# First feed-forward weights loaded through the projections' weight ring, with the token sums' helper tiles moved to other buffers

## The chip, the cores and the metric

The kernel runs on one core of one Trainium2 chip. The metric is device time of one execution in microseconds (us), the median of several runs. TensorE (PE) multiplies, VectorE (DVE) and ScalarE (ACT) do the elementwise work, GpSimd (POOL) a few small operations, and the DMAs of this kernel are issued by SyncE's queue (SP). In this kernel each engine takes its own instructions in the order of its list and waits on semaphores of the others; DMAs are waited for in the same way.

## What is computed

One decoder block on 512 tokens with 1024 channels, float32:

```
h  = rms_norm(x) ;  p = h @ w_in          (split into the parts of two mixers)
yA = sparse attention(p) ; yB = mLSTM(p)
x  = x + (sigmoid(gA) * (yA @ w_branch_a) + sigmoid(gB) * (yB @ w_branch_b)) @ w_out
h2 = rms_norm(x)
x  = x + square(relu(h2 @ w_ff1)) @ w_ff2   (w_ff1: 1024 x 4096, w_ff2: 4096 x 1024)
```

The change lies at the seam between the third and the last line: the end of `@ w_out`, the second norm, and the first columns of `h2 @ w_ff1`.

## The kernel before, in words

**Products in three matmuls.** To keep float32 precision every operand is split into a high part in the reduced format `float32r` and a low part that holds the rest. `split` (L119) does it: ACT writes the high part, DVE subtracts it from the source to get the low part. `mm3` (L114) multiplies high by high, high by low and low by high into one accumulator, so every product is three matmuls.

**Who sets the order.** The order of TensorE's instructions is the program's own (from `es_man` on): generators yield after each product, and `mix` (L260) calls events at given points of the stream. The order on ACT, DVE, POOL and SP is set by the scheduler when the program is built; then it is fixed. Tiles come from pools; a tile with `bufs=n` has n buffers that are used in turn, and who writes a buffer waits until the last reader of its former tile is done. Pools are stacked on two sides of the on-chip memory; closing a pool frees its space for the next.

**The ring.** `load_w` (L95) loads all weights of the projections up to `w_out`: one DMA of up to 512 KB into a `wraw` buffer (3 in the ring), ACT casts it to `whi`, DVE subtracts to `wlo` (4 buffers each). `hidden` (L652) also borrows a `wraw` buffer.

**The output projection.** `out_proj(c)` (L989) computes the 512 channels of half c for four tiles of 128 tokens: 8 steps of k, each `mm3`, so 24 matmuls of 512 columns a tile. Its weights are four ring tiles with two k each. After each token tile of half 1 come the residual add (L1007, DVE), the sum of squares (L1009, ACT), and `norm2` (L974): a reduce on DVE, a power on POOL, two multiplies into `hn` on DVE. `norm2_T` (L980) then transposes `hn` on TensorE (8 matmuls, tile `tpn`), splits it into `hT_h` and `hT_l` and keeps a float32 copy in `hF` (ACT, L154). It is called for token tiles 0 and 1 inside the output projection, for 2 and 3 inside the first feed-forward part.

**The feed-forward part.** The ring is closed (L1019) and four pools are opened: `ffa` (split forms of weights), `ffr` (two 512 KB landing buffers, tag `raw`), `ffu` (13 buffers `u` of [128, 1024]) and `fft` (token sums). `first_ff1` (L1050) computes the first four blocks of 128 hidden channels directly. `load_first` (L1040) loads its weights, 4 DMAs of 512 KB into the two `raw` buffers, and puts high and low parts (`w1h`, `w1l`) into `u` buffers. The products run over tokens 0 to 255 for blocks 0 to 3, then over tokens 256 to 511: 2 x 4 x 8 products, 192 matmuls of 256 columns. The events of its stream are `norm2_T(2)`, then `norm2_T(3)` and `tokens`, then `first_pair`, `load_next(6)` and `tokens4`.

All later blocks go in pairs by a seven-product scheme over halves of channels and tokens: `tokens` (L1068) forms the sums T1, T2, T3 and T4 (the last in the place of `hT`) of the normed tokens in `hF`, and the weights of a pair are turned into the forms a, s, t and b by `w1_a`, `w1_s`, `w1_t`, `w1_b` (L1104 to L1119). `products` (L1122) is `do1` to `do7`, each 12 matmuls of 256 columns: `do1` uses form a, `do2` form s with T2, `do3` form s with T1, `do4` form t with T3, then b with tokens, t with tokens, b with T4. `first_pair` (L1232) makes the forms of blocks 4 and 5; their landing tiles `w1r` and sums `w1s` are `u` buffers, those of later pairs lie in the freed `yb` pool. `ev_u` (L1033) squares and splits a finished block into a `u` buffer. `merge` (L1245) puts the second layer's `unit` (L1205: three matmuls of 512 columns, tile `fo`) between these products. Its weights come by `w2_load` (L1194): a DMA into the two `raw` buffers of `ffr`, a cast to `w2h`, a subtraction to `w2l`.

Of the kernel before, what the change touches and what calls it, by code (L numbers as in the profile page):

```python
# [20 lines left out]
S = 512  # L21
# [31 lines left out]
def hybrid_block_kernel(  # L53
# [30 lines left out]
    yb_l = ybpool.tile([128, ML_H, S], F32R, name="yb_l", tag="yb_l")  # L84
    es_ring = ExitStack()
    ring = es_ring.enter_context(pool("ring", side="right"))

    def acc(name, tag="pj", bufs=2):
        return ps.tile([128, 512], F32, name=name, tag=tag, bufs=bufs)
# [5 lines left out]
    def load_w(src, kn, c0, cn, k0=0):  # L95

        parts, kk = [], 4 if 4 * cn <= 1120 else 2
        for k in range(k0, k0 + kn, kk):
            raw = ring.tile([128, 1120], F32, name="wraw", tag="wraw", bufs=3)
            hi = ring.tile([128, 1120], F32R, name="whi", tag="whi", bufs=4)  # L100
            lw = ring.tile([128, 1120], F32R, name="wlo", tag="wlo", bufs=4)
            n = kk * cn
            nc.sync.dma_start(raw[:, :n].rearrange("p (k c) -> p k c", k=kk), src[:, k:k + kk, c0:c0 + cn])
            nc.scalar.copy(hi[:, :n], raw[:, :n])  # L104
            nc.vector.tensor_sub(lw[:, :n], raw[:, :n], hi.bitcast(F32)[:, :n])  # L105
            parts.append((hi[:, :n].rearrange("p (k c) -> p k c", k=kk),
                          lw[:, :n].rearrange("p (k c) -> p k c", k=kk)))

        def at(k, c=slice(0, cn)):
            h, l = parts[k // kk]  # L110
            return h[:, k % kk, c], l[:, k % kk, c]
        return at
# [6 lines left out]
    def split(h, l, src, scale=1.0):  # L119
        nc.scalar.activation(h, src, AF.Copy, scale=scale)  # L120
        nc.vector.tensor_sub(l, src, h.bitcast(F32))  # L121
# [530 lines left out]
    def hidden(kv, c):  # L652

        w1 = (cmp_k_w1, cmp_v_w1)[kv][0].rearrange("(k p) c -> p k c", p=128)
        raw = ring.tile([128, 1120], F32, name="wraw", tag="wraw", bufs=3)
        hi = cmpp.tile([128, 2, 256], F32R, name="w1h", bufs=3)
        lw = cmpp.tile([128, 2, 256], F32R, name="w1l", bufs=3)
        rv = raw[:, :512].rearrange("p (k c) -> p k c", k=2)
        nc.sync.dma_start(rv, w1[:, 2 * c:2 * c + 2])
        split(hi, lw, rv)  # L660
        if c == 0:
            hacc[kv] = acc("ph", "s", 2)
        p = hacc[kv]

        def go():
            for k in (2 * c, 2 * c + 1):
                lhs = fss[kv][:, k].rearrange("p a g n -> p (a g n)")
                nc.tensor.matmul(p[:, :256], lhs, hi[:, k % 2], start=k == 0, stop=False)
                nc.tensor.matmul(p[:, :256], lhs, lw[:, k % 2], start=False, stop=k == 15)
        return go  # L670
# [345 lines left out]
    esy.close()  # L1016
    qyp.close()

    es_ring.close()  # L1019

    with pool("ffa") as fa, pool("ffr") as fr, pool("ffu") as fu, pool("fft") as ft:
        UB = 13
        us = {}

        def utile(name, dt=F32R):  # L1030
            return fu.tile([128, 2 * S], dt, name=name, tag="u", bufs=UB)

        def ev_u(f, r):  # L1033

            u = utile("u").rearrange("p (a t) -> p a t", a=2)
            nc.scalar.activation(r, r, AF.Square)
            split(u[:, 0], u[:, 1], r)
            us[f] = u

        def load_first(f):  # L1040
            parts = []
            for k in (0, 4):
                raw = fr.tile([128, 4, 256], F32, name="w1raw", tag="raw", bufs=2)
                nc.sync.dma_start(raw, w_ff1[:, k:k + 4, 128 * f:128 * f + 256])
                h, l = (utile("w1" + c).rearrange("p (k c) -> p k c", k=4) for c in "hl")
                split(h, l, raw)
                parts.append((h, l))
            return lambda k, c: (parts[k // 4][0][:, k % 4, c], parts[k // 4][1][:, k % 4, c])

        def first_ff1():  # L1050

            ws = [load_first(0), load_first(2)]
            ps_ = [acc("pj", ("pj", "o")[f // 2], 2) for f in range(4)]
            for hs in (slice(0, 256), slice(256, 512)):
                for f in range(4):
                    for k in range(KT):
                        mm3(ps_[f][:, hs], *ws[f // 2](k, slice(128 * (f % 2), 128 * (f % 2) + 128)),
                            hT_h[:, k, hs], hT_l[:, k, hs], k == 0, k == KT - 1)
                        yield 3 * 256 / 2400
                    if hs.start:  # L1060
                        r = x2p.tile([128, D], F32, name="hn", bufs=2)[:, :S]
                        nc.scalar.activation(r, ps_[f], AF.Relu)
                        ev_u(f, r)
# [27 lines left out]

        def w1_load(f, first=False):
            if first:
                raw, ss = ([utile(n, F32).rearrange("p (k c) -> p k c", k=4) for _ in range(2)] for n in ("w1r", "w1s"))
            else:
                raw, ss = (ybpool.tile([128, 2, 4, 256], F32, name=n, tag=t) for n, t in (("w1r", "yb_h"), ("w1s", "yb_l")))
                raw, ss = [raw[:, 0], raw[:, 1]], [ss[:, 0], ss[:, 1]]
            for i in range(2):
                nc.sync.dma_start(raw[i], w_ff1[:, 4 * i:4 * i + 4, 128 * f:128 * f + 256])
            return raw, ss  # L1100
# [11 lines left out]

        def w1_t(w):
            (r0, r1), (sa, sb) = w
            V.tensor_sub(sb[:, :, one], r0[:, :, one], r0[:, :, two])
            V.tensor_sub(sb[:, :, two], r1[:, :, one], sa[:, :, two])
            form("t", 256, sb)

        def w1_b(w):  # L1119
            form("b", 256, w[0][1])  # L1120

        def products(f, w, nxt):  # L1122

            B = {11: (0, hi_), 21: (4, hi_), 22: (4, lo_)}
            bank = {c: acc("pj", t, 2) for c, t in (("X", "pj"), ("Y", "pj"), ("Z", "o"), ("W", "o"))}
            tmp = x2p.tile([128, 4, 256], F32, name="g2", tag="g2")
            r = x2p.tile([128, 2, S], F32, name="hn", tag="hn", bufs=2)
            X, Y, Z, W_ = (bank[c][:, :256] for c in "XYZW")
            p1, u2, t5 = tmp[:, 0], tmp[:, 1], tmp[:, 2]
            cs = {"a": one, "s1": one, "s2": two, "t3": one, "t4": two, "b1": one, "b2": two}  # L1130

            def prod(o, a, b, start):
                h, l = forms[a[0]]
                c = cs[a]
                for k in range(4):
                    if b in T:
                        bh, bl = T[b][0][:, k], T[b][1][:, k]
                    else:
                        k0, sl = B[b]
                        bh, bl = hT_h[:, k0 + k, sl], hT_l[:, k0 + k, sl]  # L1140
                    mm3(o, h[:, k, c], l[:, k, c], bh, bl, start and k == 0, k == 3, skip_group_check=not start)

            def do1():
                prod(X, "a", 11, True)
                nc.scalar.copy(p1, X)

            def do2():
                prod(Y, "s2", 2, True)
                V.tensor_add(u2, Y, p1)

            def do3():
                prod(Z, "s1", 1, True)
                V.tensor_add(t5, Z, u2)
                if w:
                    w1_a(w)
                    w1_s(w)

            def do4():
                prod(W_, "t3", 3, True)
                V.tensor_add(r[:, 1, lo_], W_, t5)  # L1160

            def do5():
                prod(X, "b1", 21, False)
                nc.scalar.activation(r[:, 0, hi_], X, AF.Relu)

            def do6():
                prod(Z, "t4", 22, False)
                V.tensor_add(r[:, 0, lo_], Z, u2)
                nc.scalar.activation(r[:, 0, lo_], r[:, 0, lo_], AF.Relu)
                ev_u(f, r[:, 0])  # L1170
                if w:
                    w1_t(w)

            def do7():
                prod(W_, "b2", 4, False)
                V.tensor_add(r[:, 1, hi_], W_, u2)
                nc.scalar.activation(r[:, 1], r[:, 1], AF.Relu)
                ev_u(f + 1, r[:, 1])
                if w:
                    w1_b(w)  # L1180
                nxt()

            return [do1, do2, do3, do4, do5, do6, do7]
# [53 lines left out]
        def after_norm():  # L1237
# [2 lines left out]

        mix(Stream(first_ff1()), [(1.54, lambda: norm2_T(2)), (7.32, after_norm), (11.0, first_pair),
                                  (21.0, lambda: load_next(6)), (21.1, tokens4)])
        n2 = iter(order2)

        def merge(fs, n, lead=0):  # L1245
# [48 lines left out]
```

## Time and profile before

| | us |
|---|---|
| three runs, median (lowest to highest) | 812.01 (811.14 to 812.54) |
| the profiled execution, whole | 809.97 |
| its span, first to last instruction | 808.2 |
| PE busy in the span | 787.5 (97%) |
| DVE busy | 536.3 (66%) |
| ACT busy | 407.3 (50%) |
| POOL busy | 71.4 (9%) |

Besides this summary the profile has a timeline of each engine (start, duration, operation, and in brackets how long the engine idled before it and for whom), a list of waits, tables of stretches with each engine's busy time and the clock that TensorE was granted (1.00 is 2.4 GHz, 0.50 is 1.2 GHz), and for each DMA the time from issue to landing. Times on a timeline count from the start of the span. Matmuls overlap: the step from start to start is what one costs in a stream. The profiled execution is 2.0 us shorter than the median of the three timed runs, and of its 809.97 us 1.8 lie outside the span.

### The profile page before, as it was taken

How to read it: one execution, taken by the hardware profiler on the slowest of the kernel's cores; microseconds unless marked ns; L12 is line 12 of the kernel's file. 1: busy time of each engine (PE TensorE's matmuls, PEld its weight loads, DVE VectorE, ACT ScalarE, POOL GpSimd, SP SyncE). 2: the span in 40 equal slices, each digit the busy share in tenths (PEclk: the TensorE clock that was granted, in tenths of full speed). 3: DMA queues.
4: the chain of work that ended last, by engine and by line, in shares of the span. 5: the costliest groups of instructions: out<-in, count | busy, mean ns of one | idle time of the engine just before them, and what ended most of it. 6: DMA issues, size and time to landing. Idle time of an engine off the chain costs nothing.

```text
span 808.2 us, 12445 instructions
## 1 busy us (share of the span) xinstructions
PE 787.5 (97%) x4772; PEld 697.3 (86%) x4772; DVE 536.3 (66%) x1007; ACT 407.3 (50%) x746; POOL 71.4 (9%) x150
## 2 busy tenths in 40 slices
PE   6999999999999999999999989999999999999998
PEld 5978889998888888888888789999998999989886
DVE  6689796778676657764754588677665767664332
ACT  6556564554466656664423576445444444444311
POOL 2000000322122221321000000000000000000000
PEclk9999999999999999999999999999999999999999
DMA  8633231666132123212332241423233333331141
GB/s 308 195 105 92 65 105 49 191 209 182 53 92 79 52 67 92 65 53 79 124 135 68 65 157 56 137 95 105 83 101 105 105 105 105 105 105 53 53 153 56
DMA packets 66320, 84.91 MB, mean 105 GB/s; under 512 B 4063, under 2 KB 50471, under 8 KB 66132
## 3 DMA queue, kind: packets, MB, share of 16 engines
q1 hardware_dynamic: 66168, 84.03, 33.2%
q8 instruction: 37, 0.61, 0.3%
q14 instruction: 23, 0.19, 0.1%
q10 hardware_dynamic: 92, 0.09, 0.0%
HBM read 81.98 MB, written 4.75 MB: 107 GB/s over the span
## 4 chain that ended last, share of the span: by engine, by line
PE 89%; DMA 4%; DVE 3%; ACT 2%; issue 1%; POOL 1%; SPq 0%; DVEq 0%; ACTq 0%; POOLq 0%
PE pj L115 18%; PE pj L116 18%; PE pj L117 18%; PE fo L115 7%; PE fo L117 7%; PE fo L116 7%; PE ao L911 3%; PE tpP L894 2%; PE st L874 1%; PE st L873 1%; DMA bt<-rel_d 1%; DMA w2r<-in_w_ff_dram 1%; PE tpn L149 1%; PE mo L431 1%; PE mo L430 1%
## 5 line engine op out<-in xcount | busy, mean ns | idle before, releaser
L115 PE MATMUL fo<-w2h,u 128*128 128x512 f32 x256 | 100.9, 394 | 0.0
L117 PE MATMUL fo<-w2h,u 128*128 128x512 f32 x256 | 100.2, 391 | 0.0
L116 PE MATMUL fo<-w2l,u 128*128 128x512 f32 x256 | 100.0, 391 | 0.0
L115 PE MATMUL pj<-whi,hT_h 128*128 128x256 f32 (+2 forms) x288 | 84.3, 293 | 3.5 <-ACT hT_h L120 1.8
L105 DVE TENSOR_TENSOR wlo<-wraw,whi 128x1024 fp32r<-128x1024 f32 (+2 forms) x58 | 72.1, 1243 | 21.7 <-ACT whi L104 20.7
L117 PE MATMUL pj<-whi,hT_l 128*128 128x256 f32 (+2 forms) x288 | 82.2, 286 | 0.0
L116 PE MATMUL pj<-wlo,hT_h 128*128 128x256 f32 (+2 forms) x288 | 81.9, 284 | 0.0
L115 PE MATMUL pj<-hT_h,whi 128*128 128x512 f32 x192 | 80.7, 420 | 0.4 <-DVE vv L121 0.4
L116 PE MATMUL pj<-hT_l,whi 128*128 128x512 f32 x192 | 75.9, 395 | 0.0
L117 PE MATMUL pj<-hT_h,wlo 128*128 128x512 f32 x192 | 75.7, 395 | 0.0
L104 ACT CAST whi<-wraw 128x1024 fp32r<-128x1024 f32 (+2 forms) x58 | 60.9, 1050 | 27.9 <-PE pj L116 12.7
L121 DVE TENSOR_TENSOR w2l<-w2r,w2h 128x1024 fp32r<-128x1024 f32 x32 | 39.2, 1223 | 50.1 <-ACT w2h L120 50.1
L120 ACT ACTIVATE w2h<-w2r 128x1024 fp32r<-128x1024 f32 x32 | 33.9, 1060 | 60.9 <-PE fo L117 60.9
L115 PEld LDWEIGHTS pj<-whi,hT_h 128*128 128x128 f32 x288 | 55.1, 191 | 5.0 <-ACT hT_h L120 2.1
L117 PEld LDWEIGHTS fo<-w2h,u 128*128 128x128 f32 x256 | 48.1, 188 | 11.1
L116 PEld LDWEIGHTS pj<-wlo,hT_h 128*128 128x128 f32 x288 | 55.2, 192 | 0.1
L117 PEld LDWEIGHTS pj<-whi,hT_l 128*128 128x128 f32 x288 | 55.0, 191 | 0.1
L116 PEld LDWEIGHTS fo<-w2l,u 128*128 128x128 f32 x256 | 48.3, 189 | 6.6
L115 PEld LDWEIGHTS fo<-w2h,u 128*128 128x128 f32 x256 | 48.2, 188 | 6.6
L877 DVE CUSTOM_DVE_ANT_0 P<-st,bt 128x128 f32<-128x128 f32 (+1 forms) x64 | 31.1, 486 | 28.5 <-PE st L874 26.2
L120 ACT ACTIVATE ph<-tpP 128x512 fp32r<-128x512 f32 (+1 forms) x64 | 27.8, 435 | 43.2 <-PE tpP L894 42.6
L887 POOL TENSOR_SCALAR P<-P,l 128x128 f32<-128x128 f32 (+1 forms) x64 | 34.2, 553 | 110.5 <-DVE l L885 110.5
(334 smaller groups left out, 2111.7 us busy)
## 6 DMA issues: line engine op xcount, KB each, us to landing
wraw<-in_w_in_dram SPq DMA_DIRECT2D x38, 512.0 KB, 3.8
w2r<-in_w_ff_dram SPq DMA_DIRECT2D x32, 512.0 KB, 3.7
w1r<-in_w_ff_dram SPq DMA_DIRECT2D x28, 512.0 KB, 4.8
bt<-rel_d SPq DMA_DIRECT2D x16, 256.0 KB, 2.9
wraw<-in_w_out_dram SPq DMA_DIRECT2D x8, 512.0 KB, 3.7
rel_d<-rel_r SPq DMA_DIRECT2D x1, 2560.0 KB
x<-in_x_dram SPq DMA_DIRECT2D x4, 512.0 KB, 8.2
wraw<-in_cmp_k_w_dram SPq DMA_DIRECT2D x8, 256.0 KB, 3.5
```

Source lines behind the costliest of these rows:

```text
L104: nc.scalar.copy(hi[:, :n], raw[:, :n])
L105: nc.vector.tensor_sub(lw[:, :n], raw[:, :n], hi.bitcast(F32)[:, :n])
L115: nc.tensor.matmul(o, ah, bh, start=start, stop=False, **kw)
L116: nc.tensor.matmul(o, ah, bl, start=False, stop=False, **kw)
L117: nc.tensor.matmul(o, al, bh, start=False, stop=stop, **kw)
L120: nc.scalar.activation(h, src, AF.Copy, scale=scale)
L121: nc.vector.tensor_sub(l, src, h.bitcast(F32))
L149: nc.tensor.transpose(tp[:, k * 128:(k + 1) * 128], hn[:, (k0 + k) * 128:(k0 + k + 1) * 128], ident)
L877: V.tensor_tensor_reduce(P, st[:, :n], bts[h][:, c0:c0 + n], -1.0, 3e38, ALU.add, ALU.min, self.nx[:, qt:qt + 1])
L887: nc.gpsimd.tensor_scalar(self.P[i], self.P[i], self.l[:, i:i + 1], 1.0, op0=ALU.mult, op1=ALU.mult)
L894: nc.tensor.transpose(tp[:, (qt - kt) * 128:(qt - kt + 1) * 128], self.P[qt][:, kt * 128:(kt + 1) * 128], ident)
L911: nc.tensor.matmul(o[:, S - x_.shape[-1]:], vn[:, self.br, self.g, kt, :], x_, start=self.br == 0 and kt == 0 and i == 0, stop=False)
```

## The change

The ring's landing buffers `wraw` become a pool of their own (`ringr`); the ring's `whi` and `wlo` stay. `first_ff1` takes its weights by `load_w`, that is through `wraw`, `whi` and `wlo`; `load_first` is gone. The ring is closed only after the `mix` of the first part. The `u` buffers are therefore two pools: 4 in the place of `wraw` (opened once the first weights are loaded) and 9 opened when the ring is closed. `first_pair` lands its weights in the two `raw` buffers of `ffr`, and its sums go into the buffer of the norm's gain (`g2`) and, in place, into the first landing buffer. Because of that `w1_t` swaps which half of form t holds which sum for the first pair, and `products` reads the halves by the names noted in `forms`. No product, and no number of matmuls, changes.

```diff
@@
     es_ring = ExitStack()
     ring = es_ring.enter_context(pool("ring", side="right"))
+    es_raw = ExitStack()
+    ring_raw = es_raw.enter_context(pool("ringr", side="right"))
@@ load_w (and the same line in hidden)
-            raw = ring.tile([128, 1120], F32, name="wraw", tag="wraw", bufs=3)
+            raw = ring_raw.tile([128, 1120], F32, name="wraw", tag="wraw", bufs=3)
@@
-    es_ring.close()
-    with pool("ffa") as fa, pool("ffr") as fr, pool("ffu") as fu, pool("fft") as ft:
+    with pool("ffa") as fa, pool("ffr") as fr, pool("fft") as ft, ExitStack() as es_u:
         UB = 13
-        us = {}
-        def utile(name, dt=F32R):
-            return fu.tile([128, 2 * S], dt, name=name, tag="u", bufs=UB)
+        us, upools = {}, []
+        def utile():
+            i = len(us) % UB
+            return upools[i >= 4].tile([128, 2 * S], F32R, name="u", tag="u", bufs=UB - 4 if i >= 4 else 4)
@@
-        def load_first(f):
-            parts = []
-            for k in (0, 4):
-                raw = fr.tile([128, 4, 256], F32, name="w1raw", tag="raw", bufs=2)
-                nc.sync.dma_start(raw, w_ff1[:, k:k + 4, 128 * f:128 * f + 256])
-                h, l = (utile("w1" + c).rearrange("p (k c) -> p k c", k=4) for c in "hl")
-                split(h, l, raw)
-                parts.append((h, l))
-            return lambda k, c: (parts[k // 4][0][:, k % 4, c], parts[k // 4][1][:, k % 4, c])
         def first_ff1():
-            ws = [load_first(0), load_first(2)]
+            ws = [load_w(w_ff1, KT, 128 * f, 256) for f in (0, 2)]
+            es_raw.close()
+            upools.append(es_u.enter_context(pool("ffv")))
@@ w1_load
             if first:
-                raw, ss = ([utile(n, F32).rearrange("p (k c) -> p k c", k=4) for _ in range(2)] for n in ("w1r", "w1s"))
+                raw = [fr.tile([128, 4, 256], F32, name="w1raw", tag="raw", bufs=2) for _ in range(2)]
+                ss = [x2p.tile([128, 4, 256], F32, name="g2", tag="g2"), raw[0]]
@@ w1_t
-            V.tensor_sub(sb[:, :, one], r0[:, :, one], r0[:, :, two])
-            V.tensor_sub(sb[:, :, two], r1[:, :, one], sa[:, :, two])
+            a, b = (two, one) if sb is r0 else (one, two)
+            V.tensor_sub(sb[:, :, a], r0[:, :, one], r0[:, :, two])
+            V.tensor_sub(sb[:, :, b], r1[:, :, one], sa[:, :, two])
             form("t", 256, sb)
+            forms["t3"], forms["t4"] = a, b
@@ products
-            cs = {"a": one, "s1": one, "s2": two, "t3": one, "t4": two, "b1": one, "b2": two}
+            cs = {"a": one, "s1": one, "s2": two, "t3": forms["t3"], "t4": forms["t4"], "b1": one, "b2": two}
@@
         mix(Stream(first_ff1()), [(1.54, lambda: norm2_T(2)), (7.32, after_norm), (11.0, first_pair),
                                   (21.0, lambda: load_next(6)), (21.1, tokens4)])
+        es_ring.close()
+        upools.append(es_u.enter_context(pool("ffu")))
```

TensorE's order is the same in both kernels; the other engines' lists differ from the end of the output projection to the first pair's products and are alike before and after. In the changed kernel line numbers from `load_w` on are 2 higher, and in the feed-forward part 2 to 6 lower. Three places of the lists follow; the brackets name the engines or DMA semaphores that a row waits for.

ACT at the end of the output projection (`xsq` the sum of squares, `tpn` the transposed norm, `w1h` or `whi` the first feed-forward weights). Before:

```order
L1009 ACTIVATE xsq,ssp<-x_4627 128x512 [waits DVE_49,Activation_49]
L120 ACTIVATE hT_h<-tpn 128x4x128 [waits PE_49] x2
L154 COPY hF<-tpn 128x4x128 [waits DVE_49] x2
L120 ACTIVATE w1h<-w1raw 128x1024 [waits DMAHW0_49]
L1009 ACTIVATE xsq,ssp<-x_4627 128x512 [waits DVE_49,Activation_49]
L120 ACTIVATE w1h<-w1raw 128x1024 [waits DMAHW1_49,PE_49]
L120 ACTIVATE w1h<-w1raw 128x1024 [waits DMAHW1_49]
```

The same place in the changed kernel:

```order
L106 CAST whi<-wraw 128x1024 [waits DMAHW6_49,PE_49]
L122 ACTIVATE hT_h<-tpn 128x4x128 [waits PE_49] x2
L106 CAST whi<-wraw 128x1024 [waits DMAHW7_49,PE_49]
L106 CAST whi<-wraw 128x1024 [waits DMAHW1_49,PE_49]
L156 COPY hF<-tpn 128x4x128 [waits DVE_49] x2
L106 CAST whi<-wraw 128x1024 [waits DMAHW4_49,PE_49]
L122 ACTIVATE hT_h<-tpn 128x4x128 [waits PE_49] x2
L1011 ACTIVATE xsq,ssp<-x_4630 128x512 [waits DVE_49,Activation_49]
```

All four casts now stand ahead of the last sum of squares; each waits for TensorE to leave its `whi` buffer.

SP from the last load of `w_out` on (`xr` the residual rows, `w2r` the second layer's weights). Before:

```order
L103 DMA wraw<-in_w_out_dram 128x2x512 [waits DMAHW5_49,DVE_49]
L1001 DMA xr<-in_x_dram 128x512 [waits DMAHW6_49,DMAHW3_49,DVE_49]
L1001 DMA xr<-in_x_dram 128x512 [waits DMAHW7_49,DMAHW4_49,DVE_49]
L1001 DMA xr<-in_x_dram 128x512 [waits DMAHW6_49,DMAHW0_49,DVE_49]
L1044 DMA w1raw<-in_w_ff_dram 128x4x256 [waits DMAHW1_49,DVE_49]
L1044 DMA w1raw<-in_w_ff_dram 128x4x256 [waits DVE_49]
L1198 DMA w2r<-in_w_ff_dram 128x2x512 [waits DMAHW1_49,DVE_49]
L1099 DMA w1r<-in_w_ff_dram 128x4x256 [waits PE_49]
```

And in the changed kernel:

```order
L105 DMA wraw<-in_w_out_dram 128x2x512 [waits DMAHW5_49,DVE_49]
L105 DMA wraw<-in_w_ff_dram 128x4x256 [waits DMAHW6_49,DVE_49]
L105 DMA wraw<-in_w_ff_dram 128x4x256 [waits DMAHW7_49,DVE_49]
L1003 DMA xr<-in_x_dram 128x512 [waits DMAHW3_49,DMAHW0_49,DVE_49]
L105 DMA wraw<-in_w_ff_dram 128x4x256 [waits DMAHW5_49,DMAHW1_49,DVE_49]
L1003 DMA xr<-in_x_dram 128x512 [waits DMAHW4_49,DVE_49]
L1003 DMA xr<-in_x_dram 128x512 [waits DMAHW0_49,DVE_49]
L105 DMA wraw<-in_w_ff_dram 128x4x256 [waits DMAHW6_49,DVE_49]
L1196 DMA w2r<-in_w_ff_dram 128x2x512 [waits DVE_49,Activation_49]
```

The first-layer loads now stand among the residual rows, and the first load of `w2r` waits for DVE and ACT where it waited for a DMA and DVE. Earlier on the same list, ahead of these rows, stand the two loads into `w1raw` in both kernels, of blocks 0 and 1 before, of blocks 4 and 5 in the change.

DVE in the change, from the last `hT_l` on (`hF` rows are the token sums, `fsl`, `ftl` the low parts of forms s and t):

```order
L1113 TENSOR_TENSOR w1raw<-w1raw,g_5349 128x4x128 [waits DVE_49]
L123 TENSOR_TENSOR fsl<-g_5349,fsh 128x1024 [waits Activation_49]
L1065 TENSOR_TENSOR hF<-hF 128x4x256 [waits Activation_49]
L123 TENSOR_TENSOR ftl<-w1raw,fth 128x1024 [waits Activation_49]
L1066 TENSOR_TENSOR hF<-hF 128x4x256 [waits DVE_49]
L123 TENSOR_TENSOR T1l<-hF,T1h 128x1024 [waits Activation_49]
L1067 TENSOR_TENSOR hF<-hF 128x4x256 [waits DVE_49]
L123 TENSOR_TENSOR w2l<-w2r,w2h 128x1024 [waits DMAHW5_49,Activation_49]
L123 TENSOR_TENSOR T3l<-hF,T3h 128x1024 [waits Activation_49]
L1071 TENSOR_TENSOR hF<-hF 128x4x256 [waits DVE_49]
L123 TENSOR_TENSOR u<-hn,u 128x512 [waits Activation_49]
L123 TENSOR_TENSOR w2l<-w2r,w2h 128x1024 [waits DMAHW6_49,Activation_49]
```

The next row is `T2l`. Before, both `w2l` rows stood ahead of `fsl`; now they stand between the token sums and ahead of `T2l`.

## Rows read from the trace of the kernel before

**Rows 1.** Page, part 1: busy time, share of the span, instructions.

```profile
PE 787.5 (97%) x4772; PEld 697.3 (86%) x4772; DVE 536.3 (66%) x1007; ACT 407.3 (50%) x746; POOL 71.4 (9%) x150
```

**Rows 2.** Waits of PE: waiting line, releaser, us in total, times, longest.

```profile
PE ph L669 <- DVE w1l L121: 2.7, 2, 1.7
...
PE pj L116 <- DVE hT_l L121: 1.7, 1, 1.7
PE pj L115 <- ACT cva L380: 1.7, 1, 1.7
PE pj L117 <- DVE w1l L121: 1.4, 2, 1.2
```

**Rows 3.** Table of stretches: length, busy us (instructions) by engine, granted clock, DMA share, GB/s.

```profile
456.90:494.13 37.23, 33.46 (x258) 32.11 (x257) 30.36 (x36) 25.39 (x38) 0.55 (x1) 0.95 0.44 142
472.70:476.00 3.30, 1.25 (x7) 0.86 (x7) 3.30 (x6) 3.30 (x6) 0.00 (x0) 0.97 0.34 129
476.00:479.30 3.30, 3.30 (x18) 3.30 (x17) 3.30 (x4) 1.58 (x3) 0.00 (x0) 0.51 0.12 30
...
62.00:66.00 4.00, 2.33 (x12) 1.70 (x11) 4.00 (x6) 3.59 (x5) 0.00 (x0) 1.00 0.34 110
180.00:184.00 4.00, 2.29 (x16) 1.86 (x15) 4.00 (x10) 2.55 (x6) 0.09 (x1) 1.00 0.29 81
```

**Rows 4.** Timeline of PE from the output projection's end to the first second-layer matmul.

```profile
451.58 0.40 PE L117 MATMUL pj<-whi,mx_l 128*128 128x512 f32 x1
...
456.67 0.40 PE L117 MATMUL pj<-whi,mx_l 128*128 128x512 f32 x1
...
458.98 0.39 PE L117 MATMUL pj<-hT_h,w1l 128*128 128x256 f32 x1 [1.21 <-DVE w1l L121]
...
461.09 1.04 PE L149 MATMUL tpn<-ident,hn 128*128 128x128 f32 x8
461.89 0.37 PE L115 MATMUL pj<-hT_h,w1h 128*128 128x256 f32 x1
...
473.23 0.38 PE L115 MATMUL pj<-hT_h,w1h 128*128 128x256 f32 x1 [0.31 <-ACT hT_h L120]
475.35 0.39 PE L116 MATMUL pj<-hT_l,w1h 128*128 128x256 f32 x1 [1.74 <-DVE hT_l L121]
...
475.81 0.41 PE L116 MATMUL pj<-hT_l,w1h 128*128 128x256 f32 x1
...
479.22 0.28 PE L117 MATMUL pj<-hT_h,w1l 128*128 128x256 f32 x1
...
488.06 0.28 PE L117 MATMUL pj<-hT_h,w1l 128*128 128x256 f32 x1
...
494.13 0.40 PE L115 MATMUL fo<-w2h,u 128*128 128x512 f32 x1
```

**Rows 5.** Timeline of DVE in the same stretch.

```profile
454.36 1.28 DVE L121 TENSOR_TENSOR hT_l<-tpn,hT_h 128x512 fp32r<-128x512 f32 x2
...
475.81 0.68 DVE L1116 TENSOR_TENSOR w1s<-w1r,w1s 128x512 f32<-128x512 f32 x1
476.41 1.22 DVE L121 TENSOR_TENSOR w2l<-w2r,w2h 128x1024 fp32r<-128x1024 f32 x1
477.55 1.22 DVE L121 TENSOR_TENSOR fsl<-w1s,fsh 128x1024 fp32r<-128x1024 f32 x1
```

**Rows 6.** Timeline of ACT in the same stretch.

```profile
456.16 1.06 ACT L120 ACTIVATE w1h<-w1raw 128x1024 fp32r<-128x1024 f32 x1
...
480.52 0.63 ACT L1036 ACTIVATE hn<-hn 128x512 f32<-128x512 f32 x1
```

**Rows 7.** DMAs from issue to landing: tile w2r, then the page's list.

```profile
DMA to landing us min/median/max: 3.5/3.7/5.3
...
x<-in_x_dram SPq DMA_DIRECT2D x4, 512.0 KB, 8.2
wraw<-in_w_out_dram SPq DMA_DIRECT2D x8, 512.0 KB, 3.7
```

More of the change, by code (lines that the diff above doesn't have):

```diff
@@ L654, in hidden @@
         w1 = (cmp_k_w1, cmp_v_w1)[kv][0].rearrange("(k p) c -> p k c", p=128)
-        raw = ring.tile([128, 1120], F32, name="wraw", tag="wraw", bufs=3)
+        raw = ring_raw.tile([128, 1120], F32, name="wraw", tag="wraw", bufs=3)
         hi = cmpp.tile([128, 2, 256], F32R, name="w1h", bufs=3)
@@ L1017, in hybrid_block_kernel @@
     qyp.close()
-    es_ring.close()
-    with pool("ffa") as fa, pool("ffr") as fr, pool("ffu") as fu, pool("fft") as ft:
+    with pool("ffa") as fa, pool("ffr") as fr, pool("fft") as ft, ExitStack() as es_u:
         UB = 13
-        us = {}
-        def utile(name, dt=F32R):
-            return fu.tile([128, 2 * S], dt, name=name, tag="u", bufs=UB)
+        us, upools = {}, []
+        def utile():
+            i = len(us) % UB
+            return upools[i >= 4].tile([128, 2 * S], F32R, name="u", tag="u", bufs=UB - 4 if i >= 4 else 4)
         def ev_u(f, r):
-            u = utile("u").rearrange("p (a t) -> p a t", a=2)
+            u = utile().rearrange("p (a t) -> p a t", a=2)
             nc.scalar.activation(r, r, AF.Square)
```

## The prediction

> **What bounds the kernel now.** I read the page's busy times first [rows 1]: PE is busy for 787.5 of 808.2 us, and what it does is the same in both kernels, so only the 20 us in which it stands, and its clock, can be gained. The list of PE's waits [rows 2] says where it stands. The last two of its large waits in program order, 1.4 us for `w1l` and 1.7 us for `hT_l`, lie at the seam that the diff touches; the others come earlier. So I went to PE's timeline there [rows 4]. The reader is to see that the last matmul of the output projection starts at 456.67, that the stream then breaks at 458.98 and at 475.35, and that the first second-layer matmul (`fo`) starts at 494.13. The table of stretches [rows 3] adds what the waits hide: after the pauses around 473 to 475 the granted clock is 0.51, that is 1.2 GHz, for 3.3 us. There the 16 steps from 475.81 to 479.22 take 0.213 us each; the 75 steps from 479.22 to 488.06 take 0.118 [rows 4].
>
> **What the seam costs now.** From 456.90 (456.67 and one step of 0.23) to 494.13 are 37.2 us. Work in it: 192 matmuls of the first four blocks and 48 of `do1` to `do4`, at 0.118 us 28.3 us, and two groups of 8 transposes at 0.80 us each (461.09 to 461.89 [rows 4]), 1.6 us: 29.9 us. So 7.3 us are lost: 3.6 us of waits (1.21, 1.74 and 0.31 in [rows 4], two of 0.2), 1.5 us of clock (16 steps times 0.095), and a rest of 2.2 us, mostly restarts, in which the first matmul after a pause takes 0.22 us and the loads of weights are late.
>
> **What the change removes.** The casts of the first weights. Before, the first cast stands on ACT behind the copies of tile 1 and starts at 456.16 [rows 6], so `w1l` is late (458.98 [rows 4]), and the last two weight tiles wait for two landing buffers. Now three of the four DMAs go out when the `w_out` weights leave `wraw`, 15 us or more ahead, and land unseen. A `whi` buffer comes free when the last token tile has passed its two k: k 0 and 1 at 451.98 (start 451.58 and 0.40 [rows 4]), k 6 and 7 at 457.07. The first cast thus runs from 452.1 to 453.2 (1.06 us [rows 6]), its subtraction when DVE is free at 454.36 [rows 5], to 455.6; behind it on DVE are the two `hT_l` of tile 1 (1.2 us), done at 456.8, and the second subtraction, done at 458.0, which PE wants at 458.6. So PE goes through at 456.90 without a stop. The fourth tile is the last to come: its DMA needs the first tile's `wraw`, so it goes out at 455.65, lands after 3.7 us [rows 7] at 459.4, its cast ends at 460.5 and its subtraction at 461.7; PE wants it at 465. The order of the lists, not their length, is what moves: DVE and ACT issue nearly the same rows.
>
> **What ends last then.** PE runs 192 matmuls, 16 transposes and `do1` without a break and is at `do2` at 456.90 + 204 x 0.118 + 1.6 = 482.5. `do2` needs `T2l`, and that is at the end of a chain on DVE. From 460.5 on DVE has no gap; the steps are 0.60 us for 512 elements and 1.14 for 1024 [rows 5] (475.81 to 476.41, 476.41 to 477.55). In order: the fourth `wlo` 1.14, two `hT_l` 1.21, the reduce 0.15, `fal` 0.60, `fbl` 1.14, two `hn` multiplies 1.33, three sums of form s and t 1.82, two `hT_l` of tile 3 1.21, the fourth sum 0.60, `fsl` 1.14, the token sum b11 1.14, `ftl` 1.22 to its end: 12.7 us, so `ftl` ends at 473.2. The second `hT_l` of tile 3 is done at 469.3, and PE wants it at 470 or later: the wait of 1.74 us is gone too, by about a microsecond.
>
> Then a wait that the change adds. The first `w2r` lands in the buffer that form t was made in, so its DMA can go out only after `ftl`, at 473.2. It lands 3.7 us later [rows 7], at 477.0; the cast of `w2h` on ACT ends at 478.1. Behind this cast on ACT stand a square (0.63 us [rows 6]) and T3's cast, done at 479.8; behind `w2l` on DVE stand `T3l`, a token sum, a `u`, the second `w2l` and `T2l`: 3 x 1.14 + 0.60 + 1.22 = 5.2 us, so `T2l` is there at 485.0. ACT has T2's high part at 483.4. PE does one matmul in between and otherwise stands from 482.5 to 485.0, 2.3 us. From there 35 matmuls (11 of `do2` and `do3`, `do4`), 4.1 us, and 0.3 us for the restart and for the last bank of `first_ff1`, which ACT empties late: the first `fo` at 489.4. That is 4.7 us earlier than 494.13.
>
> **The clock.** The new pause is of the kind that ended at 475.35: a pause, one matmul, a longer pause, in all 2.3 us without a matmul. Of the stretches with pauses this row is the nearest: 1.25 us busy in 3.30, and the next 3.3 us at 0.51. Two pauses of 1.7 us left the clock at 1.00 (busy 2.33 and 2.29 of 4.00 [rows 3]; the waits for `cva` and `ph` [rows 2]). I take the nearer row: the clock falls again and costs its 1.5 us again. The Trainium skill speaks otherwise (TensorE: Matmul & The Clock Gate, section Why this matters for your kernels): among the causes of a drop it names only pauses longer than this one, and by it the new pause would cost itself alone; here the trace does not agree, since the clock fell after pauses no longer. That case is rival 1.
>
> **The sum.** 4.7 us earlier without the clock, 1.5 us of it given back: 3.2 us. After the first `fo` both kernels do the same in the same order, and PE has no wait there before. The forms of the next pair follow `T2l` on DVE by 8.6 us, so they are there at 493.6, and their first use is 10 us after the first `fo`: no new wait. The span goes from 808.2 to 805.0 us, the profiled execution from 809.97 to 806.8. The median of the runs is 812.01, 2.0 us above that execution; taken off the median the forecast is **808.8 us**.
>
> Bounds of the unknown terms. The landing of `w2r`: 3.5 to 5.3 us [rows 7]; I take the median, 3.7, since only its own pair is in flight there. Each microsecond more is one more of pause. The landing of the fourth weight tile starts the same DVE chain, and counts in the same way. The clock: 0 or 1.5 us. That other addresses of the tiles cost nothing is an assumption; nothing in the trace speaks for a cost or a gain.
>
> **The rivals.**
>
> Rival 1, the clock holds. For it: 1.7 us did not lower it, and 2.3 is not far. Against: the stretch of 1.25 busy in 3.30. Time: 812.0 - 4.7 = 807.3 us.
>
> Rival 2, the landing is late. The pair of `w2r` goes out together, and the largest landing of this tile is 5.3 us: 1.6 us more pause, with the clock: 810.4 us, the edge of what a measurement can tell. For it: DVE and ACT have nothing else to do there that PE needs, so nothing hides it. Against: the median.
>
> Rival 3, slower than before. Two landings lie on one chain, the fourth weight tile's ahead of `wlo` and `w2r`'s ahead of `T3l`, and both engines stand in order behind them. It decides from where the two together take 4.8 us more than the 7.4 counted. At 9 us for the one and 3.7 for the other it would be 814.1 us. For it: the first loads of `x` took 8.2 us [rows 7]. Against: they were issued with many others in flight, and no landing of `w2r` passed 5.3.
>
> Rival 4, the change gives all it could: the pause at `do2` doesn't come because DVE runs ahead of my sum by 2 us. All but 0.3 us of the 7.3 are gone: 805.0 us. Against: no gap in my DVE chain is that wide.
>
> That the change doesn't do what it says would need the casts to come after 456.9 for want of a free `whi`; with the first one free at 451.98 I give that no chance of its own.
>
> **How the numbers follow.** Forecast 0.48, rival 1 0.28, rival 2 0.14, rival 3 0.05, rival 4 0.05. A measurement of this kernel can tell about 0.2% (1.6 us) from no change, so faster means below 810.4 us, slower above 813.6. Faster: 0.46 of the forecast, all of rivals 1 and 4, a little of rival 2: 0.80. Same: 0.02 of the forecast and 0.12 of rival 2: 0.14. Slower: rival 3 and the tail of rival 2: 0.06. The range goes from rival 1 with the shortest landing (807.1) to rival 2 (810.4), each with the 0.7 us by which the three runs spread about their median: 806.4 to 811.1. It leaves out rivals 3 and 4 and the ends of rival 2.
>
> **What would show it.** In the profile of the changed kernel: no wait of PE for `wlo` or `whi` after 456.67; the second pass over tokens 256 to 511 without a break and at clock 1.00; the first `fo` between 489 and 491.5; one new wait of PE, for `T2h` and `T2l`, of 2 to 3 us, with DVE's `w2l` idle before it for ACT's `w2h`, and that for the DMA `w2r`; after it 3.3 us at about 0.5. The forecast is wrong if PE stops before `do1`, if the pause at `do2` is under 1 us or over 4, or if the clock stays at 1.00 after it.

## The result, and the profile after

The changed kernel takes **804.35 us** (median of 4 runs, 803.68 to 804.51) against 811.58 us of the kernel before (median of 4 runs, 810.21 to 812.54): ratio 0.9915, 95% interval 0.9903 to 0.9927. It is faster by 7.2 us. The forecast was 808.8 us with a range of 806.4 to 811.1: the sign was right, the gain less than half of what came (3.2 of 7.2 us), and the time lies outside the range. The profiled execution takes 804.44 us (809.97 before), its span is 802.7 us. Of the runs `e0_before`, `a1_after` and `both` further down one execution each, at a mean granted clock of 0.66 to 0.76 and 963 to 1104 us, is left out; that of `a1_after` was the profiled one, so it has no seam in the table.

The page, busy times (for [rows 1]):

```profile
span 802.7 us, 12453 instructions
PE 784.9 (98%) x4772; PEld 695.7 (87%) x4772; DVE 536.3 (67%) x1007; ACT 406.6 (51%) x746; POOL 70.1 (9%) x150
```

PE is busy for 2.6 us less in a span that is 5.5 us shorter: 2.9 us of what went are time in which PE stood, and 2.6 are busy time, of which the 16 slow steps of before make 1.5. From the list of PE's waits (for [rows 2]):

```profile
PE ph L671 <- DVE w1l L123: 2.9, 2, 1.7
PE pj L117 <- ACT hT_h L122: 1.8, 1, 1.8
PE pj L117 <- ACT cva L382: 1.7, 1, 1.7
...
PE pj L117 <- ACT hn L1056: 0.5, 1, 0.5
```

The first three are the old ones outside the seam. The waits for the first weights and for `hT_l` of tile 3 are gone; one of 0.5 us is new. The stretches of the seam (for [rows 3]; length, busy us of PE, PEld, DVE, ACT and POOL, granted clock, DMA share, GB/s):

```profile
457.38:488.61 31.23, 30.75 (x257) 30.42 (x256) 29.52 (x36) 23.42 (x37) 0.86 (x1) 1.00 0.36 118
472.70:476.00 3.30, 3.30 (x30) 3.30 (x29) 3.30 (x4) 3.26 (x5) 0.00 (x0) 1.00 0.46 150
476.00:479.30 3.30, 3.30 (x30) 3.30 (x29) 3.30 (x4) 3.30 (x6) 0.00 (x0) 1.00 0.26 101
```

Where PE was busy for 1.25 us of 3.30 and then ran at 0.51, it now runs through at 1.00. PE's timeline (for [rows 4]):

```profile
457.15 0.39 PE L119 MATMUL pj<-whi,mx_l 128*128 128x512 f32 x1
457.38 0.28 PE L117 MATMUL pj<-hT_h,whi 128*128 128x256 f32 x1
...
483.38 0.28 PE L117 MATMUL pj<-T2h,fsh 128*128 128x256 f32 x1
483.59 0.39 PE L118 MATMUL pj<-T2l,fsh 128*128 128x256 f32 x1
...
487.08 0.39 PE L117 MATMUL pj<-T3h,fth 128*128 128x256 f32 x1 [0.48 <-ACT hn L1056]
...
488.61 0.40 PE L117 MATMUL fo<-w2h,u 128*128 128x512 f32 x1
```

PE goes from the output projection into the first block without a step, and from `T2h` to `T2l` in 0.21 us, where the prediction had a pause of 2.3 us. The new 0.5 us comes ahead of `do4`, whose bank is emptied late by the relu of block 3. I call **the seam** the time from the start of the last output-projection matmul to the first `fo`: 456.67 to 494.13 before, 37.46 us; 457.15 to 488.61 after, 31.46 us. So 6.0 us are won here, and 0.5 us given away in where the seam begins, which moves by up to 3 us between executions (table below). From the first `fo` to the end of the span both kernels take 314.1 us, so the gain is not made behind the seam.

Why `T2l` is in time is in the timelines of SP (with its list of waits), DVE and ACT (for [rows 5, 6]):

```profile
SPq L1196 <- DVE w1raw L1113: 14.0, 1, 14.0
...
SPq L1196 <- DVE ftl L123: 3.0, 1, 3.0
```

```profile
470.51 8.27 SPq L1196 DMA_DIRECT2D w2r<-in_w_ff_dram  x3
```

```profile
469.76 0.68 DVE L1113 TENSOR_TENSOR w1raw<-w1raw,g 128x512 f32<-128x512 f32 x1
...
472.63 1.22 DVE L123 TENSOR_TENSOR ftl<-w1raw,fth 128x1024 fp32r<-128x1024 f32 x1
...
477.17 1.22 DVE L123 TENSOR_TENSOR w2l<-w2r,w2h 128x1024 fp32r<-128x1024 f32 x1
...
482.31 1.22 DVE L123 TENSOR_TENSOR T2l<-hF,T2h 128x1024 fp32r<-128x1024 f32 x1
```

```profile
474.19 1.05 ACT L122 ACTIVATE w2h<-w2r 128x1024 fp32r<-128x1024 f32 x1
```

The first `w2r` goes out at 470.51, when the subtraction L1113 has read the second landing buffer for the last time, and not at 473.85, when `ftl` is done with the first one; it is the second `w2r` that waits for `ftl`. If the two buffers were used in turn, as the text on pools says, the first `w2r` would have got the first one, behind the two `w1raw` tiles; d8 below shows that it has the second, the one that comes free first. Its `w2h` runs from 474.19 to 475.24, `w2l` has its turn only at 477.17, and DVE has no idle time from 460.98 to 485.27.

### The profile page after: what moved, and what is told of

It reads as the page before. It is cut to its first block, busy times and chain, and to the rows that moved or that the text cites. A ratio compares the mean times of both kernels' runs of the same rounds, so it can differ in the third digit from the quotient of the medians.

```text
span 802.7 us, 12453 instructions
## 1 busy us (share of the span) xinstructions
PE 784.9 (98%) x4772; PEld 695.7 (87%) x4772; DVE 536.3 (67%) x1007; ACT 406.6 (51%) x746; POOL 70.1 (9%) x150
## 4 chain that ended last, share of the span: by engine, by line
PE 85%; DVE 6%; DMA 4%; ACT 2%; issue 2%; POOL 0%; ACTq 0%; DVEq 0%; POOLq 0%
PE pj L117 17%; PE pj L118 17%; PE pj L119 17%; PE fo L117 7%; PE fo L119 7%; PE fo L118 7%; PE ao L913 3%; DMA wraw<-in_w_in_dram 2%; PE tpP L896 2%; PE st L876 1%; PE st L875 1%; DVE wlo L107 1%; ACT whi L106 1%; DMA w1r<-in_w_ff_dram 1%; PE mo L433 1%
## 5 line engine op out<-in xcount | busy, mean ns | idle before, releaser
L117 PE MATMUL pj<-hT_h,whi 128*128 128x512 f32 (+1 forms) x256 | 98.8, 386 | 0.4 <-DVE vv L123 0.4
L118 PE MATMUL pj<-hT_l,whi 128*128 128x512 f32 (+1 forms) x256 | 94.0, 367 | 0.0
L119 PE MATMUL pj<-hT_h,wlo 128*128 128x512 f32 (+1 forms) x256 | 93.6, 366 | 0.0
L107 DVE TENSOR_TENSOR wlo<-wraw,whi 128x1024 fp32r<-128x1024 f32 (+2 forms) x62 | 76.9, 1242 | 22.9 <-ACT whi L106 21.7
L106 ACT CAST whi<-wraw 128x1024 fp32r<-128x1024 f32 (+2 forms) x62 | 65.1, 1050 | 30.6 <-PE pj L118 12.7
L119 PEld LDWEIGHTS pj<-hT_h,wlo 128*128 128x128 f32 x256 | 48.1, 188 | 8.6
L117 PEld LDWEIGHTS pj<-hT_h,whi 128*128 128x128 f32 x256 | 48.2, 188 | 7.2 <-DVE vv L123 0.6
L118 PEld LDWEIGHTS pj<-hT_l,whi 128*128 128x128 f32 x256 | 48.3, 189 | 5.5
```

Of the source, the lines that this page charges most:

```text
L117: nc.tensor.matmul(o, ah, bh, start=start, stop=False, **kw)
L118: nc.tensor.matmul(o, ah, bl, start=False, stop=False, **kw)
L119: nc.tensor.matmul(o, al, bh, start=False, stop=stop, **kw)
```

## The experiments

The theory after this reading: the seam holds 29.9 us of work (the prediction's count); the gain is the sum of two things, early first casts and an early chain of forms and T2 on DVE, plus the fall of the clock at the seam, which goes with the pause before it; and the prediction failed only in which buffer the first `w2r` waits for. The rivals are in the expectations. Each run was timed beside the kernel before (medians of 811.20, 810.91 and 810.93 us in three jobs).

| run | median us | ratio to before, 95% | seam of the profile, us |
|---|---|---|---|
| e0_before | 811.24 | 1.0001 (0.9991 to 1.0012) | 457.02 to 494.63: 37.61 |
| d8 | 805.62 | 0.9932 (0.9917 to 0.9947) | 459.15 to 490.87: 31.72 |
| castlate | 807.17 | 0.9952 (0.9940 to 0.9965) | 457.77 to 491.29: 33.52 |
| p1late | 807.37 | 0.9950 (0.9937 to 0.9962) | 456.94 to 491.55: 34.61 |
| a1_after | 804.79 | 0.9923 (0.9909 to 0.9936) | |
| both | 809.15 | 0.9980 (0.9972 to 0.9989) | 458.50 to 494.40: 35.90 |
| d32 | 807.17 | 0.9953 (0.9937 to 0.9968) | 456.20 to 489.52: 33.32 |
| swap | 803.36 | 0.9902 (0.9888 to 0.9916) | 457.86 to 488.54: 30.68 |
| a2_after | 804.15 | 0.9916 (0.9902 to 0.9931) | 456.65 to 487.36: 30.71 |
| swap2 | 804.79 | 0.9924 (0.9910 to 0.9937) | 457.60 to 488.21: 30.61 |

### e0_before: the kernel before once more

> The kernel before, unchanged. In the two profiles the changed kernel is 5.5 us shorter, in the medians 7.2 us. Theory A, the seam of the kernel before varies between executions (its waits of 1.4 and 1.7 us, and how long the clock stays at 0.5 after them): this profile has the two waits again, the clock at 0.5 again after about 473 to 475 us, and its own time may differ from 809.97 by up to 2 us, with the difference lying between 456 and 494 us. Rival B, a profiled execution of this kernel is simply shorter than a timed one: the profile is again near 810.0 with the seam as it was, and the timed runs again near 811.6 to 812.0. Median 811 to 812.5 by both.

The seam repeats (37.61 us, the same waits, clock 0.52 from 476.3 to 479.8). The executions of the kernel before differ by their mean granted clock: in the job of this run six timed executions of it at 1.000 took 810.09 to 811.35 us, three at 0.995 took 812.34 to 813.08. So theory A in part: both profiles have the fall at the seam, and the mean clock is below 1.000 in most executions but not in all. The clock is only part of the spread: the eight executions at 0.997 and 0.998 took 810.31 to 812.00 us, a median 0.7 us above that of the six at 1.000 (811.20 and 810.51). Across the jobs the medians of before are 810.9 to 811.6 us; the 812.01 that the prediction started from was a high draw of three. In two of these jobs the changed kernel was run again and gained 6.1 and 6.8 us (a1_after, a2_after), so the 7.2 are at the upper end too.

### castlate: late first casts alone

> The changed kernel, with the loads of the first feed-forward weights held back until token sums of tile 2 (first pair of loads) and tile 3 (second pair) stand, by a one-element copy into each landing buffer; the pools stay as changed. The first casts then come at about 457 us or later, as in the kernel before, and everything behind the seam keeps its new buffers. Theory A, the two parts of the change add up, and the early casts are worth only the waits at the first weights and their restarts: a wait of 1 to 2.5 us for whi/wlo near 457 to 460 is back, the second pass stays whole or nearly so, 806 to 807.5 us. Rival B, the early casts are the whole gain, because they clear ScalarE and VectorE ahead of hT and the forms: 809 to 811 us, with the wait for hT_l of tile 3 back. Rival C, the casts were never the matter: 804.9 us or less.

```diff
 def load_w(src, kn, c0, cn, k0=0, after=None):
...
+            if after is not None:
+                nc.gpsimd.tensor_copy(raw[:, :1], after)
...
-            ws = [load_w(w_ff1, KT, 128 * f, 256) for f in (0, 2)]
+            ws = [load_w(w_ff1, KT, 128 * f, 256, after=x2[:, tt, 1023:])
+                  for f, tt in ((0, 2), (2, 3))]
```

Theory A holds: 807.17 us, the first cast at 456.74 as in the kernel before ([rows 6]: 456.16), and PE's waits for `wlo` are back, the longest 0.9 us. Its timeline of ACT and list of PE's waits:

```profile
456.74 1.05 ACT L108 CAST whi<-wraw 128x1024 fp32r<-128x1024 f32 x1 [2.10 <-DMA wraw<-in_w_ff_dram]
```

```profile
PE pj L121 <- DVE wlo L109: 1.8, 3, 0.9
```

No other wait of the seam comes with them, and the clock there stays at 1.00.

### p1late: late forms alone

> The changed kernel, with the loads of the first pair's weights (w1raw, from which the forms a, s, t, b are made) held back until the normalised tile 3 stands, by a one-element copy into each landing buffer; the early casts stay. The weights land at about 469 to 472 us, as they did in the kernel before. Theory A, the forms and T2 stand in one line on VectorE and the early landing of these weights is what makes the end of the seam: no wait at the first weights, but VectorE runs dry before the forms and PE waits 2 to 4 us at do1 or do2, with or without a fall of the clock; 806.5 to 809 us. Rival B, the line has slack and the gain came from the early casts and the free ScalarE alone: 804.2 to 805.2 us.

```diff
             for i in range(2):
+                if first:
+                    nc.gpsimd.tensor_copy(raw[i][:, 0, :1], hn2[3][:, :1])
                 nc.sync.dma_start(raw[i], w_ff1[...])
```

Theory A holds: a pause at the place where the prediction had put one, of the forecast size and with a fall of the clock, but from another cause. Here the forms are late, and `w2l` stands behind `T2l` on DVE, so the landing of `w2r` has no part in it. PE's timeline and two stretches:

```profile
483.17 0.28 PE L117 MATMUL pj<-T2h,fsh 128*128 128x256 f32 x1
485.77 0.38 PE L118 MATMUL pj<-T2l,fsh 128*128 128x256 f32 x1 [2.32 <-DVE T2l L123]
```

```profile
482.90:485.80 2.90, 0.58 (x6) 0.37 (x4) 2.90 (x4) 2.77 (x5) 0.00 (x0) 1.00 0.98 328
485.80:489.40 3.60, 3.60 (x20) 3.60 (x21) 3.60 (x5) 2.58 (x5) 0.00 (x0) 0.62 0.82 263
```

One matmul, 2.32 us of nothing, then matmuls at 0.213 us a step from 486.73 to 489.93. Of its six executions five have a mean clock of 0.995 to 0.997 and take 807.10 to 807.72 us; the one at 1.000 takes 805.61. That is 1.5 to 2.1 us beside a single execution, near the 1.5 of the prediction; where the clock fell is known for the profiled one alone.

### d8 and d32: the first w2r alone comes later

> The changed kernel, with one small transfer (128 x 8 scattered numbers of w_ff2) into the buffer of the first w2r ahead of its load, so that this load goes out only when the small one has landed; VectorE's order of instructions stays that of the changed kernel, on ScalarE w2h moves one place back. It puts the landing of the first w2r at about 476.5 to 478 us, where my prediction had it (477.0) and the changed kernel did not (474.2). Theory A, the prediction's chain was right and only the buffer that the load waits for was wrong: VectorE stands idle 1.5 to 3 us before w2l, T2l is done 1.5 to 3 us later than 483.5, PE has a new wait of 1.5 to 2.5 us for T2 at do2; 806 to 807 us if the clock holds, 807.5 to 808.5 if it falls to 0.5 for 3 us behind the pause. Rival B, the two engines have slack there: under 0.5 us of wait, 804.0 to 804.9.

> As the run with 8 scattered numbers per row ahead of the first w2r, now with 32, so that the landing comes later still by the time of 24 more of them per row (the same order of instructions on every engine). There the landing was 19.0 us after the last output-projection matmul, VectorE stood 0.14 us before w2l, and PE had no wait for T2. Theory A, there is no slack left beyond that: each microsecond more of landing is one more of pause at do2, and a pause of 1.5 us or more can lower the clock to 0.5 for 3 us in some executions; with a landing 1 to 3 us later 806.5 to 809.5 us. Rival B, the scheduler's order leaves slack, PE's wait is less than half of the added landing time.

```diff
                 raw = fr.tile([128, 2, S], F32, name="w2r", tag="raw", bufs=2)
+                if i == 0:
+                    nc.sync.dma_start(raw[:, 0, :32], w_ff2[:, 30, 512:1024:16])
                 nc.sync.dma_start(raw, w_ff2[...])
```

(For d8, 8 numbers at a stride of 64.) The small transfer goes into the buffer of the first `w2r`, and in both runs it goes out when L1113 is done (472.40 in d8, 469.48 in d32), ahead of `ftl`: this is the buffer that L1113 frees. In d8 the small transfer takes 2.1 us, `w2h` starts at 478.10, 18.95 us after the start of the last output-projection matmul, and DVE loses 0.14 us. That is rival B by the wait and 31.72 us of seam, though the median of 805.62 us lies above rival B's 804.9. The changed kernel had 1.9 us of slack there (`w2h` done at 475.24, `w2l` at 477.17). Counted from the same start, the forecast's landing is at 20.33 us (477.0 - 456.67), so d8 stays 1.4 us short of it. In d32 the landing is at 20.92 us, 0.6 beyond the forecast and 2 us beyond d8, and the slack is used up. SP, ACT, DVE and PE:

```profile
469.48 0.38 SPq L1197 DMA_DIRECT2D w2r<-in_w_ff_dram  x1
473.46 6.38 SPq L1198 DMA_DIRECT2D w2r<-in_w_ff_dram  x3
477.12 1.06 ACT L122 ACTIVATE w2h<-w2r 128x1024 fp32r<-128x1024 f32 x1 [3.20 <-DMA w2r<-in_w_ff_dram]
478.21 1.23 DVE L123 TENSOR_TENSOR w2l<-w2r,w2h 128x1024 fp32r<-128x1024 f32 x1 [2.00 <-ACT w2h L122]
484.64 0.39 PE L118 MATMUL pj<-T2l,fsh 128*128 128x256 f32 x1 [1.93 <-DVE T2l L123]
```

This is the prediction's step, but for the order on ACT, where a square stands ahead of `w2h` and not behind it: DVE idle for `w2h`, `T2l` done 28.4 us after the start of the seam (forecast 28.3), a pause of 1.93 us (forecast 2.3). The gain is near the forecast too: 3.7 us (0.9953 of before), where 3.2 had been said. Theory A of d32 holds. In the profiled execution, the one of 805.29 us, the clock stayed at 1.00 after the 1.93 us; another at 1.000 took 805.49 us, four at 0.995 to 0.998 took 807.04 to 809.70. Where the clock fell in these four is not on record.

### both: do the parts add up?

> The changed kernel with both loads held back, the first feed-forward weights' (late first casts, alone a seam of 33.5 us against 31.5) and the first pair's weights' (late forms, alone 34.6 us). Theory A, the two parts of the gain add up: seam 31.5 + 2.1 + 3.1 = 36.7 us, 809 to 810.5 us, which is the kernel before but for under a microsecond. Rival B, the parts overlap, since a later start of the first blocks gives the forms the same time back: only the larger counts, seam 34.5 to 35 us, 807 to 808 us. Rival C, they are worse together, since the late casts stand ahead of the forms on ScalarE and VectorE: over 37.5 us, over 811.

The edits of castlate and p1late together. 809.15 us and a seam of 35.90 us, at a clock of 1.00 there: nearer theory A (36.7, which had p1late's fall of the clock in it) than the 35 of rival B, with both waits in PE's list:

```profile
PE pj L121 <- DVE wlo L109: 1.7, 3, 0.8
...
PE pj L120 <- DVE T2l L125: 1.2, 1, 1.2
```

Counted from a seam of the changed kernel without the wait at `do4` (a2_after, 30.71), late casts cost 33.52 - 30.71 = 2.8 us, late forms 34.61 - 30.71 = 3.9, of which 1.5 is the clock (15 steps of 0.213 instead of 0.118, and the two steps at their ends), so 2.4; their sum is 5.2, and both together cost 35.90 - 30.71 = 5.2. With the 1.5 us that the clock costs in the kernel before this gives 30.71 + 5.2 + 1.5 = 37.4 of its 37.46 us. It fits that late casts move DVE's chain as well: `T2l` is done 26.4 us after the start of the seam in a2_after, 28.0 in castlate, 28.8 in p1late and 31.6 in `both`. So the seam is accounted for in the profiled executions, to the 0.8 us by which two of the changed kernel differ. The timed ones do not confirm the last 1.5 us as the clock's: in this job five executions of `both` at a mean clock of 1.000 have a median of 809.10 us, and the two of the kernel before at 1.000 took 810.78 and 810.93. What these lose without the fall stays open.

### swap: the first w2r bound to the buffer of form t

> The changed kernel with the two landing buffers of the ring named apart, so that the first w2r is bound to the one in which form t was made and its load waits for ftl, as my prediction had it; the order that the scheduler makes of it is T3l, a u and a token sum ahead of the two w2l on VectorE, T3h and a u ahead of w2h on ScalarE. Theory A, the wait itself costs nothing once the order goes around it: the first w2r out at 473.9 and landed at 477.5, VectorE without a gap, T2l done at about 483.5, no pause at do2; 804.0 to 804.9 us. Rival B, the step as predicted: a pause of 1.5 to 2.5 us at do2, 806.5 to 808.5 us.

```diff
-                raw = [fr.tile(..., name="w1raw", tag="raw", bufs=2) for _ in range(2)]
+                raw = [fr.tile(..., name="w1raw", tag=t, bufs=1) for t in ("raw0", "raw1")]
...
-                raw = fr.tile([128, 2, S], F32, name="w2r", tag="raw", bufs=2)
+                raw = fr.tile([128, 2, S], F32, name="w2r", tag=f"raw{i % 2}", bufs=1)
```

The experiment did not do what I meant by it. The load that goes out first is again one that waits for L1113: the scheduler lets the load of the second tile pass the one that is bound to form t. SP and DVE:

```profile
471.18 3.73 SPq L1196 DMA_DIRECT2D w2r<-in_w_ff_dram  x2
480.71 2.35 DVE L123 TENSOR_TENSOR w2l<-w2r,w2h 128x1024 fp32r<-128x1024 f32 x2
```

It still tells something: the first `w2l` starts 22.9 us after the start of the seam, 2.8 us later than in the changed kernel (20.0), behind `T3l` and a token sum, and PE does not wait for T2. The 803.36 us looked like a gain over the changed kernel, so I ran the two again.

### a1_after, a2_after and swap2: how far executions differ

> The changed kernel as it is, beside the other experiments on one chip. Theory A, its executions differ only where the clock falls: 804.0 to 804.8 us median, seam (start of the last output-projection matmul to the first fo) 31.3 to 31.7 us, granted clock 1.000 at the seam in the profile; in some executions the clock falls elsewhere, after the wait at about 182 to 184 us, and those are 1.5 to 2 us longer. Rival B, its earlier runs were lucky and the clock falls at its seam too in some: median 805 to 806 us, and a profile or a run with a mean clock of 0.997 or less.

> The changed kernel as it is, again, beside the kernel with the two landing buffers named apart. Theory A: 804.0 to 805.0 us, seam about 31.5 us in the profile, with the wait of about 0.5 us for the relu of block 3 ahead of do4; single executions up to 806.5 us where the clock falls after the wait at 182 to 184 us.

> The kernel with the two landing buffers named apart, again: its profile had a seam of 30.6 us (457.86 to 488.5), 0.8 us under the changed kernel's, with no wait ahead of do4, and its runs a median of 803.36 beside 805.14. Theory A, the 0.8 us are the order (relu of block 3 ahead of the form's cast on ScalarE) and hold: the median is 0.5 to 1.2 us below that of the changed kernel on the same chip. Rival B, they are the spread between executions: the two medians lie within 0.3 us, and the seam is 31 us or more.

a2_after and swap2 give 804.15 and 804.79 us, seams of 30.71 and 30.61: theory A of swap2 fails, since the named buffers give no gain, and the medians differ the other way, by 0.6 us, within the spread of single executions (803.22 to 806.29). Rival B is right in substance and off in its bounds (0.3 us, and a seam of 31). The wait of 0.5 us ahead of `do4` is not in a2_after either: there the weights of the next pair (blocks 6 and 7) have landed in time, and the cast to their form a does not hold up the relu behind it. So it belongs to some executions, not to the kernel. No version tried here is shown to be faster than the changed kernel.

## Why the prediction was right in part and wrong in the sum

- **What the seam costs** (29.9 us of work, 7.3 lost): right. The shortest seams are 30.6 to 30.7 us, 0.7 to 0.8 above the count, of which 0.2 is the last output-projection matmul.
- **The casts of the first weights, PE through at 456.90 without a stop**: right. The first `whi` cast starts at 452.50 (forecast 452.1), the fourth tile's at 459.90 (459.4), and PE's step at 457.15 to 457.38 is 0.23 us. castlate shows that this part is worth 2.1 to 2.8 us (33.52 against 31.46 and 30.71).
- **Second pass without a break, the wait for `hT_l` of tile 3 gone**: right. Clock 1.00 in it, too.
- **The new wait**: here the prediction failed, in the sentence "The first `w2r` lands in the buffer that form t was made in, so its DMA can go out only after `ftl`, at 473.2". The load took the other of the two buffers, which is free 3.4 us earlier (470.44 against 473.85), and landed at about 474.1, not 477.0. I had named one of two buffers without a row that shows which. The pause of 2.3 us and the clock's 1.5 us of the sum hang on that step. The chain behind it was sized well: with the landing put back to 0.6 us beyond the forecast's, d32 has a pause of 1.93 us, and a gain of 3.7 us where I had forecast 3.2.
- **The clock falls again**: not so, for want of the pause that it was to follow; the clock at the seam stayed at 1.00. p1late, with a pause of 2.32 us, has the fall behind it in its profile, and a mean clock below 1.000 in five of six executions.
- **The sum**: seam forecast 34.2 us (456.67 to 489.4, and 1.5 for the clock), measured 31.46 and 30.71. Without the pause and the clock the forecast's seam is 30.4 us, and the measured 31.46 are that, the 0.5 of `do4`, and 0.5 more. The forecast's seam is 2.8 to 3.5 us too long, of the 4.4 between 808.8 and 804.35; most of the rest is the median of 812.01 that I took the gain from, which other jobs put at 810.9 to 811.6.
- **The rivals**: the time is rival 4's (805.0), given 0.05. Its case was written as luck ("DVE runs ahead of my sum by 2 us"), with "no gap in my DVE chain is that wide" against it. But the chain had such a gap: after `ftl` at 473.2 DVE has three steps of 1.14 us and is free at 476.6, while `w2l` was to start at 478.1, and behind it `T3l` was to wait 0.5 us more for ACT. These 2 us rested on the one assumption about the buffer. Measured from the start of the seam, `T2l` is done 26.4 us in (457.15 to 483.53), where the forecast had 28.3. Rival 1 could not be decided in the changed kernel, which has no such pause. In d32 the clock held after 1.93 us in the profile, in p1late it fell after 2.32: one case of each, so neither row that the prediction compared decides it.

## What to carry to other kernels

When a load waits for "a buffer of the ring", list every buffer with the time at which its last reader ends, and take the earliest that the order of loads allows; one wrong buffer in the forecast here was a load 3.4 us too late, and with it a pause of 2 us and the clock behind it. Where two loads are independent, a scheduler may let the second go first, so read the queue's order before counting on a wait. And before rejecting the best case, ask which single assumption opens the gap that speaks against it.

## What the runs showed of the hardware

**The same pause lowers the clock in one execution and not in the next.** PE waits for `w1l` near 168 and 183 us in these kernels, for up to 1.7 us. PE's timeline and the stretch behind such a wait, in the kernel before:

```profile
183.43 0.39 PE L669 MATMUL ph<-w1l,fs 128*128 128x256 f32 x1 [1.67 <-DVE w1l L121]
```

```profile
184.70:187.90 3.20, 3.13 (x25) 2.86 (x24) 2.77 (x8) 2.05 (x6) 0.00 (x0) 1.00 0.63 170
```

and in d8:

```profile
184.58 0.58 PE L671 MATMUL ph<-w1l,fs 128*128 128x256 f32 x1 [1.67 <-DVE w1l L123]
```

```profile
184.70:187.90 3.20, 3.20 (x15) 3.19 (x16) 2.63 (x9) 1.68 (x4) 0.70 (x1) 0.51 0.70 190
```

Pauses of equal length, 1.00 after the one and 0.51 (1.2 GHz) after the other. The prediction had taken "1.7 us did not lower it" as speaking for a clock that holds. It is the same with shorter pauses: e0_before and `both` each wait 0.45 us near 182 us and 1.15 us near 183.6, and behind them the clock fell to 0.50 in `both` (184 to 186 us) and held in e0_before; in castlate it fell to 0.50 (170 to 172 us) after 1.58 us. In d32 it held after 1.93. So in these traces it fell after 1.15, 1.58, 1.67, 1.74 and 2.32 us. The Trainium skill (TensorE: Matmul & The Clock Gate, section Why this matters for your kernels) warns of longer pauses between bursts of matmuls than these; the traces here do not agree. What decides between executions these runs do not show.

**Scattered numbers are slow to load.** 128 x 8 single numbers held the next load back by 2.14 us (472.40 to 474.54 in d8), 128 x 32 by 3.98 us (469.48 to 473.46 in d32), while the 512 KB of a `w2r`, in rows of 2 KB, landed 3.5 to 5.7 us after issue in the changed kernel.
